# The y operands of an output projection moved into the weight strips' tiles, and w_out's raw tiles into a pool of their own

## The chip, the core and the metric

The kernel runs on one core of a Trainium2 chip. Its metric is the device time of one execution in microseconds (us); three runs stand behind the time before. The engines that matter are TensorE (PE in the profile; its weight loads are the row PEld), VectorE (DVE), ScalarE (ACT), GpSimd (POOL) and SyncE (SP), which issues every DMA of this kernel. Each engine takes its instructions in the order in which the program lists them, and SP issues its DMAs in the same way, so an instruction or a DMA that waits holds up those behind it on its engine.

## The reference

One encoder layer is applied to 1024 prompt tokens and to 256 sample tokens, each with 16 meta tokens in front. An input projection makes queries, keys, values and gates; eight heads attend globally and eight within a neighbourhood; the gated results are joined to `y` with 2048 features, and one output projection adds to the residual.

```python
def encoder_layer(h, norm_w, w_in, ..., w_out, rope_tabs):
    u = rms_norm(h, norm_w) @ w_in.astype(h.dtype)
    qa, ka, va, za, qb, kb, vb, zb = jnp.split(u, split_points(), axis=-1)
    ...
    ya = global_gqa(qa, ka, va) * jax.nn.silu(za)
    ...
    yb = neighbourhood_attention(qb, kb, vb, rpb) * jax.nn.silu(zb)
    y = jnp.concatenate([ya, yb], axis=-1) @ w_out.astype(h.dtype)
    return h + y
```

## The kernel before

Products in full precision are made from three matmuls on split operands: `split` (line 60) copies a float32 tile to a rounded half `hi` on ACT (L61) and writes what is left, `lo`, on DVE (L62); then hi·hi, hi·lo and lo·hi are accumulated in PSUM.

The input projection runs twice, over a first chunk of 512 tokens and over a second of 784 (`chunk1`, `chunk2`). In `strips` a column strip of 128 features of `w_in` is the stationary operand. It comes in four chunks, each of which is loaded to a raw tile and split to a tile `wh` and a tile `wl` of the pool `w` (tags `wh` and `wl`, four buffers each, 2 KB in a partition). The tokens `x` (split too, 16 tiles) are the moving operand. Each triplet L210, L211, L212 takes `wh`, `wh` and `wl` as stationary and x's `hi`, `lo`, `hi` as moving operand. Attention blocks run between strips; the last eight blocks of the neighbourhood heads are what remains of `local_blocks` when the last strip of the second chunk has been made, and they run during the first pass of the output projection.

The output projection (`outproj`) is Strassen-like: seven products (passes 1, 2, 5, 6, 7, 3, 4 in this order) of halves of `y` with halves of `w_out` or sums of them (`td`, made earlier). A pass has five token tiles `t` and two column blocks `b` of 512: ten steps `n`, each of 24 matmuls in `products` (L940, L941, L942: stationary yh, yh, yl; moving wh, wl, wh). So a pass has 240 matmuls and the seven have 1680, all 128x128 by 128x512.

- Stationary operands: `y_load` brings y for one token tile and `y_operand` splits it into a tile `yo` of 8 KB (hi and lo, 8 slices of 128 columns each), of which there are three. In passes 1, 2 and 4 the DMA (L889) writes y straight into the lo half of `yo`; the other passes load y halves to `yr` and add or subtract first (L904).
- Moving operands: `w_load` brings 2 KB rows of `w_out` (or of `td`) to raw tiles `ww` (L915, L917), which before use the eight buffers of tags `wh` and `wl`; `w_operand` splits each to one of 16 tiles `wm`.
- PSUM tiles `pq` are drained by `out_sums` on ACT (passes 1 and 5) and DVE.

Pools on the right side are stacked downward from the partition's end, the others upward. In the built program the tiles lie at these bytes of each partition: the `wh` and `wl` buffers at 11,008 to 27,391; x of the first chunk at 157,440 to 222,975; x of the second chunk from 120,576; `yo` at 118,528 to 143,103; `wm` at 143,232 to 208,767. The pools `us`, `wm` and `yo` take the room of the second chunk's x, so what is written there waits for matmuls of the last strip.

A scheduler orders each engine's instructions up to the end of the first pass of the output projection; what `in_order` records from the second pass on stays in the order in which the code is written.

Of the kernel before, what the change touches and what calls it, by code (L numbers as in the profile page):

```python
# [12 lines left out]
F32 = mybir.dt.float32  # L13
F32R = mybir.dt.float32r
# [6 lines left out]
P = 128  # L21
# [13 lines left out]
ALIGN = 128  # L35
# [9 lines left out]
WCH = 4  # L45
LAG = 6
TH = (NP + NS) // 2
NT = TH // P
FB = 512
# [5 lines left out]
class Kern:  # L55
# [824 lines left out]
    def y_load(self, p, t):  # L880

        def half(i, h):
            r = self.yr.tile([P, 8, P], F32, tag="yr", name="yr")
            self.nc.sync.dma_start(r[:], self.yd[i][:, NT * h + t])
            return r[:]

        if p in (1, 2, 4):
            r = self.yo.tile([P, 2, 8, P], F32R, tag="yo", name="yo", align_bytes=ALIGN)
            self.nc.sync.dma_start(r[:, 1].bitcast(F32), self.yd[p > 1][:, NT * (p == 4) + t])  # L889
            return r  # L890
        return [half(*x) for x in {7: [(0, 0), (0, 1)], 5: [(0, 1), (1, 1)], 6: [(0, 0)], 3: [(1, 0)]}[p]]

    def y_operand(self, p, t, r):
        nc = self.nc
        if p in (1, 2, 4):
            self.split(r[:, 0], r[:, 1], r[:, 1].bitcast(F32))
            return r
        if p == 7:
            v = r[0]
            nc.vector.tensor_tensor(out=v, in0=v, in1=r[1], op=ALU.subtract)  # L900
        else:
            v = self.ysum[t][:]
            a, b, op = {5: (r[0], r[-1], ALU.add), 6: (v, r[0], ALU.subtract), 3: (r[0], v, ALU.subtract)}[p]
            nc.vector.tensor_tensor(out=v, in0=a, in1=b, op=op)  # L904
        o = self.yo.tile([P, 2, 8, P], F32R, tag="yo", name="yo", align_bytes=ALIGN)
        self.split(o[:, 0], o[:, 1], v)
        return o

    def w_load(self, p, j):

        b, k = divmod(j, 8)
        src = {1: (0, 0), 2: (8, 0), 3: (8, FH)}.get(p)
        r = self.w.tile([P, FB], F32, tag=("wh", "wl")[j % 2], name="ww")
        if src is None:
            self.nc.sync.dma_start(r[:], self.td[p][:, k, FB * b:FB * b + FB])  # L915
        else:
            self.nc.sync.dma_start(r[:], self.io["w_out"][:, src[0] + k, src[1] + FB * b:][:, :FB])  # L917
        return r
# [15 lines left out]
    def products(self, ws, y):  # L934
        nc = self.nc
        ps = self.pq.tile([P, FB], F32, tag="pq", name="pq")
        for k in range(8):
            wh, wl = ws[k][:, 0, :], ws[k][:, 1, :]
            yh, yl = y[:, 0, k, :], y[:, 1, k, :]
            nc.tensor.matmul(ps[:], yh, wh, start=k == 0, stop=False)  # L940
            nc.tensor.matmul(ps[:], yh, wl, start=False, stop=False)  # L941
            nc.tensor.matmul(ps[:], yl, wh, start=False, stop=k == 7)  # L942
        return ps[:]
# [33 lines left out]
        self.nc.sync.dma_start(self.io["y"][:, NT * h + t, FH * c + FB * b:][:, :FB], o[:])  # L977

    def outproj(self, end_attention):
        self.U, self.V = {}, {}  # L980
        order = (1, 2, 5, 6, 7, 3, 4)
        N = 2 * NT * len(order)

        def step(n):
            q, r = divmod(n, 2 * NT)
            return order[q], *divmod(r, 2)

        def tile_of(m):
            return order[m // NT], m % NT

        M = NT * len(order)
        yr, ys, wr, ws, x, out = {}, {}, {}, {}, {}, {}

        def load_y(m):
            if m < M and m not in yr:
                yr[m] = self.y_load(*tile_of(m))

        def make_y(m):
            if m < M:
                load_y(m)  # L1000
                ys[m] = self.y_operand(*tile_of(m), yr.pop(m))

        def load_w(q, j):
            if q < len(order):
                wr[q, j] = self.w_load(order[q], j)

        def make_w(q, j):
            if q < len(order):
                ws[q, j] = self.w_operand(wr.pop((q, j)))

        make_y(0)
        for j in range(8):
            load_w(0, j)
        for j in range(16):
            make_w(0, j)
            if j < 8:
                load_w(0, 8 + j)
        traced = None
        for n in range(N):
            p, t, b = step(n)  # L1020
            q, m = n // (2 * NT), n // 2
            if n == 2 * NT - 1:
                for _ in self.blocks:
                    pass
            if n == 2 * NT:
                end_attention()
                traced = len(self.nc.cur_bb.bb.instructions)
                load_y(m + 1)
            if n - 2 in out:
                self.store(out.pop(n - 2), *step(n - 2))  # L1030
            last = t == NT - 1
            if t == NT - 2 and b == 0:
                for j in range(8):
                    load_w(q + 1, j)
            if q:
                for i in (n, n + 1, n + 2):
                    if i < N and i not in x:
                        x[i] = self.x_load(*step(i))
                load_y(m + 2)
            if b == 0 and (q or not last):  # L1040
                make_y(m + 1)
            if q == 0 and last and b == 1:
                make_y(m + 1)
            ps = self.products([ws[q, 8 * b + k] for k in range(8)], ys[m])
            if last:
                for k in range(8):
                    make_w(q + 1, 8 * b + k)
                    if b == 0:
                        load_w(q + 1, 8 + k)
            o = self.out_sums(p, 2 * t + b, ps, x.pop(n, None))  # L1050
            if o:
                out[n] = o
            if n < 2 * NT:
                next(self.blocks, None)
            if traced:
                traced = self.in_order(traced)
        for n in sorted(out):
            self.store(out[n], *step(n))

    def build(self):  # L1060
# [3 lines left out]
        with tc.tile_pool(name="dr", bufs=1, space=DRAM) as dp, tc.tile_pool(name="const", bufs=1) as cp, \  # L1064
# [19 lines left out]
            with ExitStack() as ps, ExitStack() as es_y:  # L1084
                def pool(stack, name, bufs, **kw):
                    setattr(self, name, stack.enter_context(tc.tile_pool(name=name, bufs=bufs, **kw)))
# [27 lines left out]
                es_pp.close()  # L1114
                pool(es_y, "pq", 4, space=PSUM, **kw)

                for name, bufs in (("us", 2 * NT), ("wm", 16), ("yo", 3)):
                    pool(es_late, name, bufs, side="right", **kw)

                def end_attention():  # L1120
# [96 lines left out]
```

## Time and profile before

| What | Value |
|---|---|
| median of three runs | 2192.64 us (2191.17 to 2193.61) |
| profiled execution: time, span of its instructions | 2193.63 us, 2191.8 us |
| mean granted TensorE clock | 0.997 |
| PE busy | 2165.2 us of the span |
| the 1680 matmuls of the output projection | from 1788.99 us to the end |
| the last matmul of the input projection starts at | 1767.65 us |

Times in the trace count from the span's start. A row of the timeline gives start, length, engine, line, operation and operands, and in brackets the idle time before it with what ended it; lengths of matmuls are latencies and overlap, so the pace is read from one start to the next. A row of the windows gives the stretch, its length, the busy time of each engine (instructions in brackets), the granted clock, the DMA share and the rate in GB/s.

### The profile page before, as it was taken

Reading aid. Unit: us, or ns where it says so; the run is one execution under the profiler, and the core shown is the slowest. Engines: PE = TensorE matmul, PEld = TensorE weight load, DVE = VectorE, ACT = ScalarE, POOL = GpSimd, SP = SyncE. Lnnn points to the kernel's source line nnn. Section 1 sums busy time; section 2 is a strip of 40 time slices with the busy share of each in tenths; the row PEclk is TensorE's granted clock in tenths of the full one; section 3 lists DMA queues with packets and bytes.
Section 4 is the critical chain, followed back from the end, with each engine's and each line's share of the span. In section 5 each row is a group of like instructions: output and inputs, shape, how many; then the busy total and the mean of one; then the engine's idle time right before and its main releaser. Section 6 shows DMA issues by size and latency. Waiting matters only on the chain.

```text
span 2191.8 us, 34025 instructions
## 1 busy us (share of the span) xinstructions
PE 2165.2 (99%) x11736; PEld 1881.7 (86%) x11736; DVE 1646.2 (75%) x2956; ACT 1124.4 (51%) x2259; POOL 518.2 (24%) x249
## 2 busy tenths in 40 slices
PE   8999999999999999999999999999999979999999
PEld 7888888888878999999999999999989968888887
DVE  8687976778774999995899998777768775546663
ACT  7556544554464667665676665444444454232220
POOL 1232421222212223322223323422323311000000
PEclk9999999999999999999999999999999989999999
DMA  8767898988364334334333336544434363653673
GB/s 297 221 196 229 280 307 303 345 275 264 129 220 143 106 108 116 106 107 143 104 111 116 98 122 188 167 139 137 133 123 134 95 235 113 221 190 125 218 228 113
DMA packets 262173, 383.82 MB, mean 175 GB/s; under 512 B 44880, under 2 KB 113136, under 8 KB 262000
## 3 DMA queue, kind: packets, MB, share of 16 engines
q1 hardware_dynamic: 262000, 381.65, 53.9%
q8 instruction: 92, 1.51, 0.3%
q14 instruction: 81, 0.66, 0.1%
HBM read 281.01 MB, written 100.38 MB: 174 GB/s over the span
## 4 chain that ended last, share of the span: by engine, by line
PE 94%; DVE 2%; DMA 2%; ACT 1%; issue 1%; SPq 0%; POOL 0%; DVEq 0%; ACTq 0%; POOLq 0%
PE pp L210 21%; PE pp L211 21%; PE pp L212 21%; PE pq L942 6%; PE pq L941 6%; PE pq L940 6%; PE po L470 2%; PE sp L438 1%; PE sp L333 1%; PE sp L334 1%; PE sp L332 1%; PE po L374 1%; PE po L372 1%; PE po L373 1%; DMA ww<-in_w_out 0%
## 5 line engine op out<-in xcount | busy, mean ns | idle before, releaser
L210 PE MATMUL pp<-x,wh 128*128 128x512 f32 (+1 forms) x2496 | 892.4, 359 | 7.3 <-ACT wh L61 5.5
L211 PE MATMUL pp<-x,wh 128*128 128x512 f32 (+1 forms) x2496 | 888.6, 356 | 0.4 <-DVE x L159 0.4
L212 PE MATMUL pp<-x,wl 128*128 128x512 f32 (+1 forms) x2496 | 888.7, 356 | 0.0
L210 PEld LDWEIGHTS pp<-x,wh 128*128 128x128 f32 x2496 | 469.1, 188 | 71.6 <-ACT wh L61 7.0
L212 PEld LDWEIGHTS pp<-x,wl 128*128 128x128 f32 x2496 | 469.6, 188 | 60.9 <-DVE wl L62 0.7
L211 PEld LDWEIGHTS pp<-x,wh 128*128 128x128 f32 x2496 | 469.9, 188 | 59.9 <-DVE x L159 1.3
L220 POOL PARTITION_ALL_REDUCE m<-ms x78 | 225.8, 2895 | 378.2 <-ACT ms L218 333.3
L62 DVE TENSOR_TENSOR wl<-wr,wh 128x512 fp32r<-128x512 f32 (+1 forms) x290 | 213.1, 738 | 130.3 <-ACT wh L61 105.3
L61 ACT CAST wh<-wr 128x512 fp32r<-128x512 f32 (+1 forms) x290 | 174.9, 607 | 224.6 <-PE pp L211 206.7
L301 POOL PARTITION_ALL_REDUCE tot<-a x80 | 178.2, 2228 | 470.2 <-DVE a L299 455.1
L940 PE MATMUL pq<-wm,yo 128*128 128x512 f32 x560 | 222.0, 396 | 0.0
L941 PE MATMUL pq<-wm,yo 128*128 128x512 f32 x560 | 221.3, 395 | 0.0
L942 PE MATMUL pq<-wm,yo 128*128 128x512 f32 x560 | 221.0, 395 | 0.0
L284 POOL PARTITION_ALL_REDUCE ma<-m x80 | 104.6, 1307 | 423.3 <-DVE m L282 415.1
L942 PEld LDWEIGHTS pq<-wm,yo 128*128 128x128 f32 x560 | 105.5, 188 | 24.8 <-DVE yo L62 0.4
L941 PEld LDWEIGHTS pq<-wm,yo 128*128 128x128 f32 x560 | 105.6, 189 | 24.6
L940 PEld LDWEIGHTS pq<-wm,yo 128*128 128x128 f32 x560 | 105.8, 189 | 24.3
L336 ACT COPY S<-sp 128x512 f32<-128x512 f32 x136 | 78.4, 579 | 51.2 <-PE sp L334 38.9
L194 ACT CAST wh<-wr 128x512 fp32r<-128x512 f32 x132 | 81.1, 614 | 41.5 <-PE pp L211 41.4
L62 DVE TENSOR_TENSOR pl<-S,ph 128x512 fp32r<-128x512 f32 x136 | 97.9, 732 | 3.9 <-ACT ph L61 3.8
L352 DVE TENSOR_TENSOR S<-S,ma 128x512 f32<-128x512 f32 x136 | 97.1, 772 | 3.9 <-POOL ma L284 3.9
L61 ACT CAST ph<-S 128x512 fp32r<-128x512 f32 x136 | 83.2, 612 | 32.9 <-PE po L373 32.3
(199 smaller groups left out, 3298.1 us busy)
## 6 DMA issues: line engine op xcount, KB each, us to landing
wr<-in_w_in SPq DMA_DIRECT2D x414, 256.0 KB, 3.5
wld<-wl SPq DMA_DIRECT2D x132, 256.0 KB, 4.4
wl<-wld SPq DMA_DIRECT2D x132, 256.0 KB, 3.1
wq<-in_w_out SPq DMA_DIRECT2D x64, 256.0 KB, 5.2
td<-wq SPq DMA_DIRECT2D x64, 256.0 KB, 4.3
ww<-td SPq DMA_DIRECT2D x64, 256.0 KB, 4.9
yr<-yd SPq DMA_DIRECT2D x30, 512.0 KB, 5.4
ww<-in_w_out SPq DMA_DIRECT2D x48, 256.0 KB, 5.3
```

The lines of the kernel that those rows point to most:

```text
L61: self.hi = nc.scalar.copy(hi, full).ins
L62: return nc.vector.tensor_tensor(out=lo, in0=full, in1=hi.bitcast(F32), op=ALU.subtract).ins
L210: nc.tensor.matmul(p[:, :n], wh[:, k, :], xh[:, :n], start=first, stop=False)
L211: nc.tensor.matmul(p[:, :n], wh[:, k, :], xl[:, :n], start=False, stop=False)
L212: nc.tensor.matmul(p[:, :n], wl[:, k, :], xh[:, :n], start=False, stop=last)
L220: nc.gpsimd.partition_all_reduce(m2[:], ms[:], P, RED.add)
L284: nc.gpsimd.partition_all_reduce(ma[:], m1[:], P, RED.max)
L301: nc.gpsimd.partition_all_reduce(tot[:], a1[:], P, RED.add)
L352: nc.vector.tensor_tensor(out=s, in0=s, in1=mb, op=ALU.subtract)
L940: nc.tensor.matmul(ps[:], yh, wh, start=k == 0, stop=False)
L941: nc.tensor.matmul(ps[:], yh, wl, start=False, stop=False)
L942: nc.tensor.matmul(ps[:], yl, wh, start=False, stop=k == 7)
```

## The change

Three things change, with no arithmetic of the outputs changed.

1. The stationary operand of the output projection no longer lies in `yo`. Each token tile's y is split into two `wh` tiles (hi) and two `wl` tiles (lo) of the pool `w`, four slices of 128 columns in each. With four buffers of each tag there is room for two token tiles, where `yo` had three. Each split of 128x1024 becomes two of 128x512, on ACT and on DVE: 35 more of each in the program.
2. In pass 1, and for the first tile of pass 2, y is loaded straight into two `wl` tiles (L890 of the changed file), with two DMAs of 256 KB in place of one of 512 KB. Passes 2 and 4 otherwise load y through `yr`.
3. The raw tiles of `w_out` get a pool of their own, `ww`, of eight buffers of 2 KB, where `yo` had been: at bytes 126,752 to 143,135.

```diff
--- before.py
+++ after.py
@@ -884,33 +884,42 @@
             self.nc.sync.dma_start(r[:], self.yd[i][:, NT * h + t])
             return r[:]
 
-        if p in (1, 2, 4):
-            r = self.yo.tile([P, 2, 8, P], F32R, tag="yo", name="yo", align_bytes=ALIGN)
-            self.nc.sync.dma_start(r[:, 1].bitcast(F32), self.yd[p > 1][:, NT * (p == 4) + t])
-            return r
-        return [half(*x) for x in {7: [(0, 0), (0, 1)], 5: [(0, 1), (1, 1)], 6: [(0, 0)], 3: [(1, 0)]}[p]]
+        if self.yr is None:
+            los = [self.w.tile([P, WCH, P], F32R, tag="wl", name="yl") for _ in range(2)]
+            for i, l in enumerate(los):
+                self.nc.sync.dma_start(l[:].bitcast(F32), self.yd[p > 1][:, t, WCH * i:WCH * i + WCH])
+            return los
+        return [half(*x) for x in {7: [(0, 0), (0, 1)], 5: [(0, 1), (1, 1)], 6: [(0, 0)], 3: [(1, 0)], 2: [(1, 0)], 4: [(1, 1)]}[p]]
 
     def y_operand(self, p, t, r):
         nc = self.nc
-        if p in (1, 2, 4):
-            self.split(r[:, 0], r[:, 1], r[:, 1].bitcast(F32))
-            return r
-        if p == 7:
+        if len(r[0].shape) == 3 and r[0].shape[1] == WCH:
+            his, los, full = [], r, [l[:].bitcast(F32) for l in r]
+            for l, f in zip(los, full):
+                his.append(self.w.tile([P, WCH, P], F32R, tag="wh", name="yh"))
+                self.split(his[-1][:], l[:], f)
+            return his, los
+        if p in (2, 4):
+            v = r[0]
+        elif p == 7:
             v = r[0]
             nc.vector.tensor_tensor(out=v, in0=v, in1=r[1], op=ALU.subtract)
         else:
             v = self.ysum[t][:]
             a, b, op = {5: (r[0], r[-1], ALU.add), 6: (v, r[0], ALU.subtract), 3: (r[0], v, ALU.subtract)}[p]
             nc.vector.tensor_tensor(out=v, in0=a, in1=b, op=op)
-        o = self.yo.tile([P, 2, 8, P], F32R, tag="yo", name="yo", align_bytes=ALIGN)
-        self.split(o[:, 0], o[:, 1], v)
-        return o
+        his, los = [], []
+        for i in range(2):
+            his.append(self.w.tile([P, WCH, P], F32R, tag="wh", name="yh"))
+            los.append(self.w.tile([P, WCH, P], F32R, tag="wl", name="yl"))
+            self.split(his[i][:], los[i][:], v[:, WCH * i:WCH * i + WCH])
+        return his, los
 
     def w_load(self, p, j):
 
         b, k = divmod(j, 8)
         src = {1: (0, 0), 2: (8, 0), 3: (8, FH)}.get(p)
-        r = self.w.tile([P, FB], F32, tag=("wh", "wl")[j % 2], name="ww")
+        r = self.ww.tile([P, FB], F32, tag="ww", name="ww")
         if src is None:
             self.nc.sync.dma_start(r[:], self.td[p][:, k, FB * b:FB * b + FB])
         else:
@@ -936,7 +945,7 @@
         ps = self.pq.tile([P, FB], F32, tag="pq", name="pq")
         for k in range(8):
             wh, wl = ws[k][:, 0, :], ws[k][:, 1, :]
-            yh, yl = y[:, 0, k, :], y[:, 1, k, :]
+            yh, yl = (a[k // WCH][:, k % WCH, :] for a in y)
             nc.tensor.matmul(ps[:], yh, wh, start=k == 0, stop=False)
             nc.tensor.matmul(ps[:], yh, wl, start=False, stop=False)
             nc.tensor.matmul(ps[:], yl, wh, start=False, stop=k == 7)
@@ -977,7 +986,7 @@
         self.nc.sync.dma_start(self.io["y"][:, NT * h + t, FH * c + FB * b:][:, :FB], o[:])
 
     def outproj(self, end_attention):
-        self.U, self.V = {}, {}
+        self.U, self.V, self.yr = {}, {}, None
         order = (1, 2, 5, 6, 7, 3, 4)
         N = 2 * NT * len(order)
 
@@ -1114,7 +1123,7 @@
                 es_pp.close()
                 pool(es_y, "pq", 4, space=PSUM, **kw)
 
-                for name, bufs in (("us", 2 * NT), ("wm", 16), ("yo", 3)):
+                for name, bufs in (("us", 2 * NT), ("wm", 16), ("ww", 8)):
                     pool(es_late, name, bufs, side="right", **kw)
 
                 def end_attention():
```

Line numbers of the changed file are 9 higher from `w_load` on (L917 there is L926, L940 is L949).

The scheduler makes another order of it around the end of the input projection. On SP, the rows from the last strip's end: in the program before, six raw loads of `w_out` (`ww`) stand ahead of the load of the next head's keys (`kfull`), and two more directly ahead of it.

```order
1220 L917 DMA ww<-in_w_out 128x512 x2
1221 L773 DMA zd_138<-zt 128x272
1222 L917 DMA ww<-in_w_out 128x512 x4
1223 L319 DMA yd_166<-y 128x4x64
1224 L917 DMA ww<-in_w_out 128x512 x2
1225 L778 DMA kfull<-kfd_78 128x240
1226 L779 DMA kfull<-k2d_148 128x784
1227 L780 DMA kfull<-kfd_78 128x16
1228 L789 DMA qfull<-qfd_122 128x240
1229 L790 DMA qfull<-q2d_164 128x784
```

In the changed program the same place on SP reads as follows (`yl` are the y loads; one more stands just ahead of these rows).

```order
1221 L773 DMA zd_138<-zt 128x272
1222 L890 DMA yl<-yd_165 128x512 x2
1223 L319 DMA yd_166<-y 128x4x64
1224 L926 DMA ww<-in_w_out 128x512 x3
1225 L778 DMA kfull<-kfd_78 128x240
1226 L779 DMA kfull<-k2d_148 128x784
1227 L780 DMA kfull<-kfd_78 128x16
1228 L494 DMA vn_88<-vl 128x4x128
1229 L478 DMA bt<-in_bt 128x1152
1230 L494 DMA vn_88<-vl 128x2x128
1231 L499 DMA vn_88<-vl 16x128
1232 L789 DMA qfull<-qfd_122 128x240
```

Three y loads stand where six raw loads stood, all raw loads come after the last strip, and the query load `qfull` stands behind the loads and stores of `vn` and `bt`.

On PE, the rows behind the last strip's transposes: before, the scores (`sp`) and the weighted sums (`po`) of attention come ahead of the first matmul of the output projection (`pq`).

```order
9513 L438 MATMUL sp<-qfull,kfull 128x128 x2
9514 L438 MATMUL sp<-qfull,kfull 128x192 x2
9515 L272 MATMUL sp<-q,km 112x256
9516 L273 MATMUL sp<-q,km 112x256
9517 L438 MATMUL sp<-qfull,kfull 128x128 x2
9518 L272 MATMUL sp<-q,km 112x256
9519 L273 MATMUL sp<-q,km 112x256
9520 L438 MATMUL sp<-qfull,kfull 128x192 x2
9521 L467 MATMUL po<-Pm,vm_271 128x256
9522 L470 MATMUL po<-S,vw 128x128 x2
9523 L470 MATMUL po<-S,vw 128x192 x2
9524 L940 MATMUL pq<-wm,yo 128x512
```

In the changed program nine of them, three slices of y, come first (the last four of the nine are shown), and these rows follow.

```order
9518 L951 MATMUL pq<-wm,yl 128x512
9519 L949 MATMUL pq<-wm,yh 128x512
9520 L950 MATMUL pq<-wm,yh 128x512
9521 L951 MATMUL pq<-wm,yl 128x512
9522 L438 MATMUL sp<-qfull,kfull 128x128 x2
9523 L438 MATMUL sp<-qfull,kfull 128x192 x2
9524 L467 MATMUL po<-Pm,vm_271 128x256
9525 L470 MATMUL po<-S,vw 128x128 x2
9526 L470 MATMUL po<-S,vw 128x192 x2
9527 L272 MATMUL sp<-q,km 112x256
9528 L949 MATMUL pq<-wm,yh 128x512
9529 L273 MATMUL sp<-q,km 112x256
```

The projection's matmuls have moved ahead of attention there and in between, and the block's weighted sums stand ahead of the next block's second scores.

On DVE, the softmax of the block whose weighted sums these are (`m` its maxima, `ma` their maximum over the partitions, `a` its sums, `Pm` its meta probabilities). Before:

```order
2404 L452 TENSOR_TENSOR m_20200<-S 128x256
2405 L62 TENSOR_TENSOR q<-qfull,q 128x1024
2406 L62 TENSOR_TENSOR wm<-ww,wm 128x512
2407 L455 TENSOR_TENSOR m_20200<-m_20200,S 128x128
2408 L62 TENSOR_TENSOR wm<-ww,wm 128x512 x2
2409 L282 TENSOR_TENSOR m_20200<-m_20200,Sm 16x256
2410 L276 SCALAR_TENSOR_TENSOR Sm<-sp,Sl 48x256
2411 L443 SCALAR_TENSOR_TENSOR S<-sp,bt 128x256
2412 L443 SCALAR_TENSOR_TENSOR S<-sp,bt 128x384
2413 L62 TENSOR_TENSOR wm<-ww,wm 128x512 x2
2414 L459 TENSOR_TENSOR S<-S,ma 128x256
2415 L462 TENSOR_TENSOR S<-S,ma 128x384
```

In the changed program:

```order
2406 L62 TENSOR_TENSOR wm<-ww,wm 128x512
2407 L282 TENSOR_TENSOR m_20200<-m_20200,Sm 16x256
2408 L62 TENSOR_TENSOR wm<-ww,wm 128x512
2409 L784 TENSOR_TENSOR km<-kfull,km 128x48
2410 L459 TENSOR_TENSOR S<-S,ma 128x256
2411 L462 TENSOR_TENSOR S<-S,ma 128x384
2412 L289 TENSOR_TENSOR Sm<-Sm,ma 48x256
2413 L452 TENSOR_TENSOR a_20214<-S 128x256
2414 L455 TENSOR_TENSOR a_20214<-a_20214,S 128x128
2415 L294 TENSOR_TENSOR Pm<-Sm,Pm 16x256
2416 L299 TENSOR_TENSOR a_20214<-a_20214,Sm 16x256
2417 L62 TENSOR_TENSOR q<-qfull,q 128x1024
```

The split of the next head's queries, which needs the `qfull` load, stood between the first two steps of this softmax (L452, L455) and now stands behind its last (L299).

## The prediction

> **What bounds the kernel now.** I read the page first, then the windows of the stretch in which PE is not full, then PE's timeline there, then its pace from one matmul's start to the next.
>
> ```profile
> span 2191.8 us, 34025 instructions
> PE 2165.2 (99%) x11736; PEld 1881.7 (86%) x11736; DVE 1646.2 (75%) x2956; ACT 1124.4 (51%) x2259; POOL 518.2 (24%) x249
> PE 94%; DVE 2%; DMA 2%; ACT 1%; issue 1%; SPq 0%; POOL 0%; DVEq 0%; ACTq 0%; POOLq 0%
> ```
>
> PE carries 94% of the chain that ended last, so only two things can move the time: PE's idle time, and the pace of its matmuls. The windows show where it idles.
>
> ```profile
> 1760.00:1780.00 20.00, 13.16 (x77) 11.65 (x75) 11.81 (x23) 9.55 (x20) 0.16 (x1) 0.83 0.69 226
> 1780.00:1800.00 20.00, 14.84 (x67) 12.59 (x68) 17.88 (x39) 11.23 (x22) 3.95 (x3) 0.83 0.90 329
> 1853.00:1909.00 56.00, 56.00 (x242) 45.40 (x242) 26.81 (x39) 13.43 (x20) 0.00 (x0) 1.00 0.58 193
> ```
>
> Between the last strip and the output projection PE misses 6.84 + 5.16 = 12.0 us, at a granted clock of 0.83 and with the DMA engines up to 0.90 busy. From 1853 us, in passes 2 to 7 of seven, PE is full at clock 1.00, and DVE (26.81 of 56) and ACT (13.43) have room. PE's rows of the gap:
>
> ```profile
> 1762.90 1.26 PE L470 MATMUL po<-S,vw 128*128 128x128 f32 x8
> ...
> 1771.90 0.55 PE L491 MATMUL tp<-ident,vt 128*128 128x128 f32 x3 [2.19 <-ACT vl L493]
> 1776.49 2.47 PE L438 MATMUL sp<-qfull,kfull 128*128 128x128 f32 x8 [4.05 <-DMA qfull<-q2d]
> ...
> 1781.87 0.68 PE L438 MATMUL sp<-qfull,kfull 128*128 128x128 f32 x4 [2.48 <-DVE S L443]
> ...
> 1786.73 0.58 PE L467 MATMUL po<-Pm,vm 128*128 128x256 f32 x1 [3.29 <-DVE Pm L294]
> 1787.11 2.33 PE L470 MATMUL po<-S,vw 128*128 128x128 f32 x8
> 1788.99 0.88 PE L940 MATMUL pq<-wm,yo 128*128 128x512 f32 x1
> ```
>
> Four stalls, 2.19 + 4.05 + 2.48 + 3.29 = 12.01 us, are the whole gap, and all stand ahead of the first `pq`. Then the pace, of the input projection (39 matmuls of 512 columns in a row, the last row being the first of the next kind) and of pass 2 (its first matmul and that of pass 3, 240 later):
>
> ```profile
> 405.22 0.39 PE L210 MATMUL pp<-x,wh 128*128 128x512 f32 x1
> ...
> 414.06 0.38 PE L210 MATMUL pp<-x,wh 128*128 128x496 f32 x1
> ```
> ```profile
> 1853.05 0.39 PE L940 MATMUL pq<-wm,yo 128*128 128x512 f32 x1
> ...
> 1908.81 0.39 PE L940 MATMUL pq<-wm,yo 128*128 128x512 f32 x1
> ```
>
> The first is 8.84 / 39 = 226.7 ns a matmul, the second 55.76 / 240 = 232.3 ns: the same shape, as many weight loads, the same order of hi and lo, the same distance of 2 KB between the moving hi and lo, but 5.7 ns more. What I find different is where the stationary operand lies: the strips' at 11 to 27 KB of the partition with x far above, `yo` at 119 to 143 KB just under `wm`.
>
> **The change part by part.**
>
> *Stationary operand.* After the change `yh` and `yl` lie in the very buffers of `wh` and `wl`, and `wm` stays within the range of x. If place sets the pace, `pq` should run as `pp`: passes 2 to 7 have 1440 matmuls, 1440 x 5.67 ns = 8.2 us, all on the path since PE is full there. The ends are 0 (place is nothing) and 8.2 for these passes; no stretch of 512-column matmuls in the trace is lastingly slower with the stationary operand low, so I see no loss. I take 8.2, since the nearest rows are those of the same buffers. Pass 1 shares PE with attention, after which the strips too need some ten matmuls to reach their pace, so of its 240 x 5.67 = 1.4 us I take 0.4 (ends 0 and 1.4).
>
> A rule of the Trainium skill speaks against this term: "TensorE: Matmul & The Clock Gate", section "Step-by-step: what each phase is for", says that PE has two independent read ports into SBUF, so that loading the next weights takes no read bandwidth from the running matmul; no place of an operand would then matter. The trace has two paces at one clock for one shape, which that rule does not explain.
>
> *The gap.* Before, y is loaded and split last of all:
>
> ```profile
> 1758.23 5.01 SPq L917 DMA_DIRECT2D ww<-in_w_out  x4
> ...
> 1767.88 0.80 SPq L917 DMA_DIRECT2D ww<-in_w_out  x2
> ...
> 1771.10 0.43 SPq L790 DMA_DIRECT2D qfull<-q2d  x1
> ...
> 1776.42 2.44 SPq L917 DMA_DIRECT2D ww<-in_w_out  x4
> ...
> 1780.55 0.45 SPq L889 DMA_DIRECT2D yo<-yd  x1
> ```
> ```profile
> 1774.72 0.42 DVE L452 TENSOR_TENSOR m<-S 128x256 f32<-128x256 f32 x1
> 1777.50 1.23 DVE L62 TENSOR_TENSOR q<-qfull,q 128x1024 fp32r<-128x1024 f32 x1 [2.36 <-ACT q L61]
> ...
> 1779.25 0.28 DVE L455 TENSOR_TENSOR m<-m,S 128x128 f32<-128x128 f32 x1
> ...
> 1788.23 1.57 DVE L62 TENSOR_TENSOR yo<-yo 128x1024 fp32r<-128x1024 f32 x1
> ```
>
> The y load goes out at 1780.55 and its lo half is ready at 1789.80, so no `pq` could fill a stall. And DVE holds the softmax of the block at work for 4.53 us (1774.72 to 1779.25) behind a split of q that waits for `qfull`; that softmax ends in the `Pm` on which the fourth stall waits. After the change the y loads take the places of six raw loads from 1753 us on, since `wl` tiles are free then; y is split before the strip ends; the q split stands behind the softmax; and `pq` matmuls stand between the pieces of attention. The third and fourth stalls then have work to cover them and one of their causes is gone: 2.48 + 3.29 = 5.77 us saved. The first two I leave at 6.24. Nine `pq` matmuls (2.1 us) fill part of the second, but `qfull` is now issued behind `vn` and `bt`, some 2 to 3 us later by the seven issues of about 0.4 us between. What is late next is `qfull`.
>
> Against it: all 16 raw loads now wait for the last strip (the old place of 1767.88), where six had gone before. At the rate of the gap's second window 256 KB take 0.80 us (262 KB / 329 GB/s), so six take 4.8; but five of the six y halves that were loaded in that crowd leave it or come later, which gives nearly as much back. So the ends of this part are -12.0 (all stalls filled) and +4.8 (raw loads simply late); I take -5.8, which the stalls' own rows carry.
>
> *The clock.* The eight L470 after the fourth stall take 2.33 us, those at 1762.90 took 1.26. With that stall filled they should run at full clock: 1.07, I take 1.0 (ends 0, and 2.5 with the slow L438 too).
>
> *Splits in halves, two y tiles in place of three.*
>
> ```profile
> L62 DVE TENSOR_TENSOR wm<-ww,wm 128x512 fp32r<-128x512 f32 x85 | 53.9, 687 | 6.3 <-ACT wm L61 6.0
> L61 ACT CAST wm<-ww 128x512 fp32r<-128x512 f32 x83 | 48.9, 620 | 19.7 <-DMA ww<-td 10.8 <-DMA ww<-in_w_out 3.6 <-PE pq L942 3.5
> L62 DVE TENSOR_TENSOR yo<-ysum,yo 128x1024 fp32r<-128x1024 f32 x15 | 18.4, 1226 | 40.5 <-ACT yo L61 40.5
> L61 ACT CAST yo<-ysum 128x1024 fp32r<-128x1024 f32 x15 | 15.7, 1049 | 89.0 <-DVE ysum L904 89.0
> yo<-yd SPq DMA_DIRECT2D x4, 512.0 KB, 3.6
> ```
>
> Two halves cost DVE 2 x 687 - 1226 = 148 ns more a tile and ACT 2 x 620 - 1049 = 191 ns: 35 tiles, 5.2 and 6.7 us, hidden in the room named above. With two tiles, y of tile t+1 can be written only when PE has left tile t-1, which leaves one tile's 48 matmuls, 11.2 us. In pass 1 the load waits as well: 3.6 + 1.24 + 1.37 = 6.2 us against 11.2. Later passes load to `yr` ahead. I take 0; a shallower buffer gives no gain, and without the cover it is at most the 6.2 us once in a pass. SP queues nothing new there but the y load itself, with stores of attention's y behind it, which nobody needs for two steps.
>
> *Sum.* -8.2 - 0.4 - 5.8 - 1.0 = -15.4 against the profiled execution's own 2193.6 (span 2191.8 and 1.8 around it; 1.0 above the median of 2192.64): 2178.2, so 2178 us. A measurement tells changes of about 0.2%, 4.4 us, from none.
>
> **The rivals.**
>
> - *Place is nothing.* Only the gap shrinks: 2193.6 - 6.8 = 2187. For it: attention's rows cannot be told apart by place, and something unseen may set the two paces. Against it: after each interruption the strips return to 226.7, and `pq` never does in 335 us. By the rule on the two ports this is what would come out. Chance 0.25.
> - *The pace alone.* The late raw loads eat what the filled stalls give: 2193.6 - 8.6 = 2185. For it: DMA share 0.90 in the gap. Chance 0.15.
> - *All stalls go.* -12.0 - 2.0 - 8.6: 2171. Against it: `qfull` comes later, and PE's first score needs it. Chance 0.05.
> - *Slower: raw weights behind the last strip, and no pace.* `ww` now lies where x was, so the first load waits for the strip's last matmuls; PE has `pq` matmuls ahead of attention in its order, so each late raw tile holds attention up too. Price +4.8: 2198. It decides when the sixteenth raw load lands later than its 24 matmuls can be fed, that is if the gap's DMA stays at 0.90 for over 5 us longer. Chance 0.08.
>
> **How the numbers follow.** The forecast as summed has 0.47. Around it I see 4 us either way (2174 to 2182). Taking in the rivals at 2185 and 2187 with as much uncertainty, and little beyond, 2172 to 2191 leaves out half of the rival at 2171 and the one at 2198, and the tails. Faster by over 0.2% (under 2188.3): 0.45 of the forecast, 0.16 of place-is-nothing, 0.11 of pace-alone and 0.05: 0.77. Slower: 0.05 of the last rival and 0.02 of tails: 0.07. The rest, 0.16, is within 0.2%.
>
> **What would show it.** The first matmuls of passes 2 and 3 should lie 54.4 us apart, not 55.8; passes 2 to 7 are then right. The first `pq` should start within 8 us of the last `pp`, with a stall on `qfull` and none on `Pm`; the two windows after the last strip should miss 6 us of PE, not 12. DVE's and ACT's splits of y must end no wait of PE in passes 2 to 7. A pace still at 232 ns refutes the first term; waits of `pq` for `wm` of more than 3 us refute the second.

## The result

The changed kernel took 2185.25 us (median of six executions, 2184.67 to 2187.12) against 2193.8 us of the kernel before (six executions, 2191.17 to 2194.68): a ratio of 0.9964, 95% interval 0.9954 to 0.9975. That is faster by some 8 us, and the forecast had 15.4: 2185 lies in the range, but the change is little more than half of what was forecast.

The profile after, first the page's head and chain, then the windows in the columns used before:

```profile
span 2183.9 us, 34132 instructions
PE 2164.4 (99%) x11736; PEld 1881.0 (86%) x11736; DVE 1647.3 (75%) x2991; ACT 1127.1 (52%) x2294; POOL 520.6 (24%) x249
PE 95%; DMA 1%; DVE 1%; ACT 1%; SPq 0%; issue 0%; POOL 0%; DVEq 0%; ACTq 0%; POOLq 0%
```

```profile
1760.00:1780.00 20.00, 14.55 (x79) 11.76 (x77) 12.23 (x28) 9.21 (x20) 5.16 (x3) 0.90 0.68 227
1780.00:1800.00 20.00, 20.00 (x93) 17.04 (x93) 17.33 (x37) 10.07 (x21) 3.19 (x2) 0.93 0.93 324
```

In the two windows behind the last strip PE now misses 5.45 us, where it missed 12.0. PE's rows of that stretch, and of the first matmuls of passes 2 and 3:

```profile
1769.59 0.52 PE L491 MATMUL tp<-ident,vt 128*128 128x128 f32 x3 [1.07 <-DVE vt L246]
1770.17 0.50 PE L949 MATMUL pq<-wm,yh 128*128 128x512 f32 x1
1770.90 0.50 PE L950 MATMUL pq<-wm,yh 128*128 128x512 f32 x1 [0.23 <-DVE wm L62]
...
1773.35 0.50 PE L950 MATMUL pq<-wm,yh 128*128 128x512 f32 x1 [0.30 <-DVE wm L62]
1773.69 0.40 PE L951 MATMUL pq<-wm,yl 128*128 128x512 f32 x1
1777.77 2.47 PE L438 MATMUL sp<-qfull,kfull 128*128 128x128 f32 x8 [3.68 <-DMA qfull<-q2d]
1779.78 0.67 PE L467 MATMUL po<-Pm,vm 128*128 128x256 f32 x1
1780.25 2.34 PE L470 MATMUL po<-S,vw 128*128 128x128 f32 x8
...
1845.34 0.39 PE L949 MATMUL pq<-wm,yh 128*128 128x512 f32 x1
...
1901.10 0.39 PE L949 MATMUL pq<-wm,yh 128*128 128x512 f32 x1
```

Of the four stalls two are gone, the one on `Pm` and the one on `S`; the first is 1.07 in place of 2.19, the one on `qfull` 3.68 in place of 4.05, and two short waits for `wm` are new: 5.28 us in all against 12.01. But passes 2 and 3 still begin 55.76 us apart, 232.3 ns a matmul. The pace did not move at all.

In what follows two lengths are read from each trace: from the start of the last `pp` to the start of pass 2 (the gap and pass 1), and from there to the start of the last matmul (passes 2 to 7). Before they are 85.40 and 334.63 us, after 78.88 and 334.39. So 6.5 us came from the gap and pass 1, and 0.2 from the rest. The last `pp` itself starts at 1766.46 after and 1767.65 before, but this moves between 1766.46 and 1768.27 over the runs below without order among them (e3_x128, which slows the strips, apart), so some 1 us of the profiled difference is scatter.

### The profile page after: what moved, and what is told of

It reads as the page before. It is cut to its first block, busy times and chain, and to the rows that moved or that the text cites. A ratio compares the mean times of both kernels' runs of the same rounds, so it can differ in the third digit from the quotient of the medians.

```text
span 2183.9 us, 34132 instructions
## 1 busy us (share of the span) xinstructions
PE 2164.4 (99%) x11736; PEld 1881.0 (86%) x11736; DVE 1647.3 (75%) x2991; ACT 1127.1 (52%) x2294; POOL 520.6 (24%) x249
## 4 chain that ended last, share of the span: by engine, by line
PE 95%; DMA 1%; DVE 1%; ACT 1%; SPq 0%; issue 0%; POOL 0%; DVEq 0%; ACTq 0%; POOLq 0%
PE pp L210 21%; PE pp L211 21%; PE pp L212 21%; PE pq L949 6%; PE pq L951 6%; PE pq L950 6%; PE po L470 2%; PE sp L438 2%; PE sp L333 1%; PE sp L334 1%; PE sp L332 1%; PE po L372 1%; PE po L374 1%; PE po L373 1%; PE tp L491 0%; DMA xr<-in_x 0%
## 5 line engine op out<-in xcount | busy, mean ns | idle before, releaser
L61 ACT CAST wh<-wr 128x512 fp32r<-128x512 f32 (+1 forms) x290 | 174.9, 607 | 226.7 <-PE pp L211 201.2
L949 PE MATMUL pq<-wm,yh 128*128 128x512 f32 x560 | 221.6, 396 | 0.2
L950 PE MATMUL pq<-wm,yh 128*128 128x512 f32 x560 | 220.9, 395 | 0.5 <-DVE wm L62 0.5
L951 PE MATMUL pq<-wm,yl 128*128 128x512 f32 x560 | 221.3, 395 | 0.0
L950 PEld LDWEIGHTS pq<-wm,yh 128*128 128x128 f32 x560 | 105.5, 188 | 25.7 <-DVE wm L62 1.4
L949 PEld LDWEIGHTS pq<-wm,yh 128*128 128x128 f32 x560 | 105.6, 189 | 25.0 <-ACT wm L61 0.9
L951 PEld LDWEIGHTS pq<-wm,yl 128*128 128x128 f32 x560 | 105.5, 188 | 24.4
```

The costliest lines, as they stand in the source:

```text
L61: self.hi = nc.scalar.copy(hi, full).ins
```

## Experiments on the pace

The forecast's first term rested on where y lies. It left open what else differs between the strips' matmuls and the projection's. The tiles' addresses, told with the kernel before, hold one more difference: every 512-column matmul of the strips has both its operands at a multiple of 256 bytes of the partition (x from 157,440 and 120,576, `wh` from 11,008), while in the projection `wm` starts at 143,232, an odd multiple of 128, and y at a multiple of 256 (118,528 before, 11,008 after).

**e1_wm256: the changed kernel with wm at a multiple of 256.**

```diff
-        w = self.wm.tile([P, 2, FB], F32R, tag="wm", name="wm", align_bytes=ALIGN)
+        w = self.wm.tile([P, 2, FB], F32R, tag="wm", name="wm", align_bytes=256)
```

> The changed kernel with one edit: the tiles wm (the moving operand of the output projection) start at a multiple of 256 bytes of the partition (143,104) and not at an odd multiple of 128 (143,232). In the program every 512-column matmul of the input projection has its moving operand at a multiple of 256, every one of the output projection at an odd multiple of 128. Theory A (this start sets the pace): the first matmuls of passes 2 and 3 lie 54.4 us apart, not 55.8; 1440 x 5.67 ns = 8.2 us and some 0.5 of pass 1 go: 2185.3 - 8.7 = 2176.5 us. Theory B (the pace comes of something in the stream itself, such as its groups of 24 matmuls or the traffic beside it): 55.8 us a pass, 2185 us.

Measured: 2177.45 us, ratio to the kernel before 0.9921 (0.9907 to 0.9934). The first matmuls of passes 2 and 3 on PE's timeline:

```profile
1845.72 0.39 PE L949 MATMUL pq<-wm,yh 128*128 128x512 f32 x1
...
1900.12 0.39 PE L949 MATMUL pq<-wm,yh 128*128 128x512 f32 x1
```

They are 54.40 us apart, 226.7 ns a matmul, and passes 2 to 7 take 326.17 us: 8.22 less, the size of the forecast's first term to a tenth, but for a move of 128 bytes in place of some 100 KB. Theory B falls.

**e2_before_wm256: the same edit in the kernel before.**

> The kernel before with the same edit; yo, which is stacked under wm, moves by 128 bytes too, so its stationary operands now start at an odd multiple of 128. Theory A, moving operand alone: 2193.8 - 8.7 = 2185 us, 54.4 us a pass, although y lies high in the partition. If the start of the stationary operand counted in the same way: 55.8 us a pass and 2194. Theory C (both the low place of y and the start of wm are needed): 2194, while the run on the changed kernel reaches 2176.5.

Measured: 2194.43 us, ratio 1.0004 (0.9995 to 1.0013).

```profile
1852.70 0.40 PE L940 MATMUL pq<-wm,yo 128*128 128x512 f32 x1
...
1908.70 0.40 PE L940 MATMUL pq<-wm,yo 128*128 128x512 f32 x1
```

56.00 us a pass, 233.3 ns a matmul. Since `yo` is stacked under `wm`, it had moved by 128 bytes too: `wm` at a multiple of 256, `yo` not. So the moving operand alone does not decide; either the stationary one counts in the same way, or a low place of y is needed as well. The next runs part these.

**e4_series: 19 series of 96 matmuls, one thing varied at a time.** After the kernel's end this is added (`low` are two tiles of the pool `w`, `top` two tiles at 223 KB, `g` the moving operand):

```diff
+            for j, (mo, so, d, n, high) in enumerate(SERIES):
+                for _ in range(4):
+                    ps = self.pq.tile([P, FB], F32, tag="pq", name=f"m{chr(97 + j)}")
+                    for i in range(24):
+                        k, r = divmod(i, 3)
+                        x = mo // 4 + 1024 * k + (d // 4 if r == 1 else 0)
+                        y = so // 4 + P * (k % 3)
+                        nc.tensor.matmul(ps[:, :n], flat[high][r // 2][:, y:y + P], g[:, x:x + n], start=i == 0, stop=i == 23)
```

> The changed kernel with 19 series of 96 matmuls each behind its end, in the form of the projection's (triplets hi, hi, lo over eight slices, groups of 24), in which one thing varies at a time: start of the moving operand (0, 128, 0, 64, 32, 192 bytes past a multiple of 256), start of the stationary operand (0, 128), its place (11 to 27 KB, 223 KB), the distance of moving lo from hi (2048, 2176 bytes), the columns (512, 496, 272, 256, 128). The time of the whole says nothing. Theory A: 226.7 ns a matmul with the moving operand at 0, 232.3 at 128, whatever the stationary operand's start and place; lo alone at 128 in between. Theory B: all series of 512 columns at one pace. My place theory: the series with stationary high at 232, low at 226.7, whatever the start.

A row of PE's timeline holds a whole series here, so from one start to the next are 96 matmuls. In order (`mb` on): moving at 128; 0; 64; 32; 192; stationary at 128; both at 128; both at 0 with y high; moving at 128 with y high; lo 128 bytes off; the last row closes it.

```profile
2223.79 22.55 PE L1089 MATMUL mb<-mv,st 128*128 128x512 f32 x96
2246.18 21.94 PE L1089 MATMUL mc<-mv,st 128*128 128x512 f32 x96
2267.95 22.15 PE L1089 MATMUL md<-mv,st 128*128 128x512 f32 x96
2289.94 22.55 PE L1089 MATMUL me<-mv,st 128*128 128x512 f32 x96
2312.33 22.56 PE L1089 MATMUL mf<-mv,st 128*128 128x512 f32 x96
2334.72 22.56 PE L1089 MATMUL mg<-mv,st 128*128 128x512 f32 x96
2357.12 21.94 PE L1089 MATMUL mh<-mv,st 128*128 128x512 f32 x96
2378.90 21.93 PE L1089 MATMUL mi<-mv,st 128*128 128x512 f32 x96
2400.67 22.55 PE L1089 MATMUL mj<-mv,st 128*128 128x512 f32 x96
2423.06 22.55 PE L1089 MATMUL mk<-mv,st 128*128 128x512 f32 x96
2445.45 21.61 PE L1089 MATMUL ml<-mv,st 128*128 128x496 f32 x96
```

By differences of starts over 96: moving at 128 past a multiple of 256 (`mb`) 233.2 ns, at 0 (`mc`) 226.8, at 64 (`md`) 229.1, at 32 and 192 (`me`, `mf`) 233.2; stationary at 128 alone (`mg`) 233.3; both at 128 (`mh`) 226.9. The place is nothing either way: with y high 226.8 where the starts agree (`mi`) and 233.2 where they don't (`mj`), with y low 226.8 and 233.2. Moving the lo half alone by 128 (`mk`) gives the slow pace too, 233.2, not one in between as theory A had it. So theory A needs another form: what counts is whether the two starts are equal modulo 256, for the moving hi and lo alike.

**e4b_series: other pairs of starts.** The same code with another list.

> The changed kernel with 18 other series of 96 matmuls behind its end; moving and stationary start past a multiple of 256, in pairs: 0 and 0, 256 and 0, 512 and 0, 0 and 256, 64 and 64, 32 and 32, 160 and 32, 64 and 192, 16 and 0, 96 and 0, 64 and 0, 160 and 0, 224 and 0, 0 and 64, 0 and 192; then 0 and 0 with lo 64 bytes further from hi, and 384 columns with 128 and 0, 0 and 0. The time of the whole says nothing. Equality modulo 256 as the rule: 226.7 ns for the first six (with 256 and 0 alike), 233 for 160 and 32 and for 64 and 192, between 227 and 233 for the others. If equality modulo 512 were the rule, 256 and 0 as well as 0 and 256 run at 233.

```profile
2226.29 21.92 PE L1089 MATMUL mb<-mv,st 128*128 128x512 f32 x96
2248.05 21.92 PE L1089 MATMUL mc<-mv,st 128*128 128x512 f32 x96
2269.81 21.92 PE L1089 MATMUL md<-mv,st 128*128 128x512 f32 x96
2291.57 21.97 PE L1089 MATMUL me<-mv,st 128*128 128x512 f32 x96
2313.38 21.95 PE L1089 MATMUL mf<-mv,st 128*128 128x512 f32 x96
2335.17 22.55 PE L1089 MATMUL mg<-mv,st 128*128 128x512 f32 x96
2357.56 22.46 PE L1089 MATMUL mh<-mv,st 128*128 128x512 f32 x96
2379.85 22.40 PE L1089 MATMUL mi<-mv,st 128*128 128x512 f32 x96
```

Moving and stationary at 256 and 0, 512 and 0, 0 and 256 (`mb`, `mc`, `md`): 21.76 us, 226.7 ns each, so equality modulo 512 is not needed. 64 and 64, 32 and 32 (`me`, `mf`): 227.2 and 227.0, a transient at their start included. 160 and 32, 64 and 192 (`mg`, `mh`), which differ by 128: 233.2 and 232.2. In the rows behind these the same list gives 231.7 at a difference of 16 bytes, 229.1 at 64, 233.4 at 96, 234.1 at 160, 233.2 at 192 and 233.4 at 224, and 232.1 with the lo half alone 64 bytes off. The first series of each list, which starts behind a long idle stretch, took 251.9 and 250.2 and is left out. In the other 25 series of 512 columns the fast pace goes with starts that are equal modulo 256, and with no others; only a difference of 64 between the two operands comes near it.

**e10_yo128: the kernel before, with yo moved down by 128 bytes.**

```diff
-                for name, bufs in (("us", 2 * NT), ("wm", 16), ("yo", 3)):
+                for name, bufs in (("us", 2 * NT), ("wm", 16), ("shift", 1), ("yo", 3)):
                     pool(es_late, name, bufs, side="right", **kw)
+                    if name == "shift":
+                        self.shift.tile([P, 32], F32, name="shift")
```

> The kernel before with one edit: yo moves down by 128 bytes (118,400 in place of 118,528), so that the stationary operand too starts at an odd multiple of 128, as wm does. Theory A, second form (what counts is that the starts of the two operands are equal modulo 256, from the series behind e4_series and from e2_before_wm256, where moving wm alone moved yo with it): 54.4 us a pass, 2193.8 - 8.7 = 2185 us, with y as high in the partition as before. Theory A, first form (the moving operand has to start at a multiple of 256): 2194. Theory C (a low place of y is needed too): 2194.

Measured: 2184.29 us, ratio 0.9957 (0.9944 to 0.9971).

```profile
1852.49 0.39 PE L940 MATMUL pq<-wm,yo 128*128 128x512 f32 x1
...
1906.89 0.39 PE L940 MATMUL pq<-wm,yo 128*128 128x512 f32 x1
```

54.40 us a pass with y as high as ever and both operands at odd multiples of 128. The second form of theory A holds in the kernel itself; the first form and theory C fall. All four pairs have now run at full length: `wm` and y at 128 and 0 (the kernels before and after) and at 0 and 128 (e2_before_wm256) are slow, 0 and 0 (e1_wm256) and 128 and 128 are fast. The spacer of 128 bytes is worth as much as the whole change under study.

**e3_x128: the strips of the first chunk made slow.**

```diff
+                    pool(es_1, "shift", 1, side="right")
+                    self.shift.tile([P, 32], F32, name="shift")
                     pool(es_1, "x", 16, side="right")
```

> The changed kernel with x of the first chunk moved by 128 bytes, so that 960 matmuls of 512 columns and 1536 of 496 in the input projection take their moving operand from odd multiples of 128 bytes; the second chunk (2496 of 512 columns) stays at multiples of 256, and so does the stationary operand. Theory A: the 960 go from 226.7 to 232.3 ns, 5.4 us, and the 1536 of 496 columns by 3 to 6 ns, 5 to 9 us: 2195 to 2200 us. Theory B: 2185.

Measured: 2194.92 us, 9.7 more than the changed kernel (ratio to the kernel before 1.0005, 0.9996 to 1.0014). The first row below is the first of a run of 512-column matmuls, the second its 37th:

```profile
407.69 0.40 PE L210 MATMUL pp<-x,wh 128*128 128x512 f32 x1
...
416.09 0.40 PE L210 MATMUL pp<-x,wh 128*128 128x512 f32 x1
```

36 matmuls take 8.40 us, 233.3 ns each, where the same stretch had 226.7. The last matmul of the first chunk starts at 616.77 us, where in the changed kernel it starts at 607.08: 9.7 us later, all of what was measured. From there to the last `pp` of the second chunk, which was not touched, it is 1159.6 us against 1159.4. The effect can be switched on where it was off as well as off where it was on.

## Experiments on the gap

**e5_raw_only: the raw tiles' pool alone, y high as before, two tiles.**

```diff
-        r = self.w.tile([P, FB], F32, tag=("wh", "wl")[j % 2], name="ww")
+        r = self.ww.tile([P, FB], F32, tag="ww", name="ww")
...
-                for name, bufs in (("us", 2 * NT), ("wm", 16), ("yo", 3)):
+                for name, bufs in (("us", 2 * NT), ("wm", 16), ("ww", 8), ("yo", 2)):
```

> The kernel before with the changed kernel's pool of eight raw tiles at the same bytes (126,752 to 143,135), and y in yo as before, two tiles deep in place of three, under it (110,336 to 126,720). The start of both operands modulo 256 stays as before (128 and 0), so the pace stays at 55.8 us a pass. On SP and DVE the order is that of the changed kernel (the split of q behind the softmax, raw loads behind the last strip), but y is loaded late, so no pq stands between the pieces of attention. Theory G1 (the gap shrinks because y is there early and pq matmuls fill it): the four stalls stay near 12 us, 2192 to 2198 us. Theory G2 (it shrinks because DVE's softmax no longer waits behind the split of q): the stall on Pm goes (3.3 us) and part of the one on S, 2188 to 2190 us. If both: 2190 with pq's first start some 3 us earlier than before.

Measured: 2201.79 us, ratio 1.0036 (1.0024 to 1.0049). The gap and pass 1 take 83.57 us, 1.8 less than before; passes 2 to 7 take 342.67, 8 more. PE's waits from 1850 us on (a row gives who waited for what, the us in total, how often, and the longest):

```profile
PE pq L940 <- ACT yo L61: 2.5, 2, 1.4
PE pq L942 <- DVE yo L62: 2.3, 3, 1.3
PE pq L941 <- DVE wm L62: 0.4, 2, 0.2
```

So two tiles are not free by themselves. Where y is loaded straight into the tile, the load waits for PE to leave it (the y loads of these passes, L889, wait 50.3 us for L942), and PE then waits for the splits. The rows hold 5.2 of the 8 us; where the rest goes, no row of waits shows. No stall on `Pm` is left in the gap, as G2 says, but that on `qfull` has grown to 8.78 us, and little is won: each theory held half.

**e12_raw_yr: the same with passes 2 and 4 loading y through yr.**

```diff
-        if p in (1, 2, 4):
+        if self.yr is None:
             r = self.yo.tile([P, 2, 8, P], F32R, tag="yo", name="yo", align_bytes=ALIGN)
...
+        if p in (2, 4):
+            v = r[0]
+        elif p == 7:
```

> e5_raw_only (yo high, two tiles deep, raw tiles in their own pool; 2201.8 us, of which some 8 us more than before in passes 2 to 7) with the changed kernel's way of loading y in passes 2 and 4, through yr. If the 8 us come of two tiles of y whose load waits for PE to leave them: passes 2 to 7 take 334.5 us again, 2193.5 us, and what is left beside the kernel before is the gap alone. If two tiles are too few anyhow: above 2197 us.

Measured: 2191.63 us, ratio 0.9989 (0.9980 to 0.9998). Passes 2 to 7 are back at 334.39 us, so the 8 us were the direct loads into two tiles, and `yr` covers them. The gap and pass 1 take 83.73 us; PE's waits in it:

```profile
PE sp L438 <- DMA qfull<-q2d: 8.6, 1, 8.6
PE sp L438 <- DVE S L443: 1.3, 1, 1.3
PE tp L491 <- DVE vt L246: 1.1, 1, 1.1
```

The order on DVE took the stall on `Pm` away, yet the stalls add up to 11.0 us, since `qfull`, now issued behind `vn` and `bt` (its second load at 1774.48, where before it went out at 1771.10), takes up what `Pm` gave.

**e13_ylate: the changed kernel with the loads of y late.** In pass 1 they are tied behind the eighth raw load on SP; `make_y(0)` moves behind the raw loads in the code for this.

```diff
-                self.nc.sync.dma_start(l[:].bitcast(F32), self.yd[p > 1][:, t, WCH * i:WCH * i + WCH])
+                with self.tc.issue_after(self.lastww):
+                    self.nc.sync.dma_start(l[:].bitcast(F32), self.yd[p > 1][:, t, WCH * i:WCH * i + WCH])
```

> The changed kernel with one thing undone: the loads of y in pass 1 are tied on SP behind the eighth raw load of w_out, so y is there late although its tiles are free early. Everything else stays: y low in the partition, two tiles deep, splits in halves, passes 2 and 4 through yr, raw tiles in their own pool. PE's order ahead of the first pq is then again that of the kernel before. Theory G1 (about 4.9 of the 6.5 us that the gap and pass 1 lost come of y being there early, the rest of the order on DVE and SP): from the last pp to pass 2 83.7 us as in e12_raw_yr, 2185.3 + 4.9 = 2190 us. If the low place or the halves themselves bring the 4.9 us: 78.9 us, 2185.3 us.

Measured: 2192.38 us, ratio 0.9996 (0.9987 to 1.0005). The gap and pass 1 take 84.90 us, so 6.0 of the 6.5 us are lost again, more than the 4.9 of G1, and the gain of the whole change is gone. PE's waits from 1760 us to 2190:

```profile
PE sp L438 <- DMA qfull<-q2d: 8.2, 1, 8.2
PE sp L438 <- DVE S L443: 1.7, 2, 1.3
PE tp L491 <- DVE vt L246: 1.1, 1, 1.1
PE pq L952 <- ACT yh L61: 0.8, 1, 0.8
```

The first loads of y go out at 1781.47 here, later still than in the kernel before (1780.55), and the last row, 0.8 us, is a wait for their split; so the 6.0 overstate the worth of early y a little, and 5 to 6 us is what e12_raw_yr, whose gap and pass 1 are 4.85 us longer than the changed kernel's, and this run bear out. In the changed kernel two of the loads stand in this row, ahead of the last `pp` at 1766.46:

```profile
1757.11 4.54 SPq L890 DMA_DIRECT2D yl<-yd  x2
```

What the low place buys is time, not pace: there y can be loaded while the last strip still reads x, and with y at hand PE has `pq` matmuls to do while `qfull` is on its way.

**e8_best: e1 with the raw tiles out of x's range.**

```diff
-                for name, bufs in (("us", 2 * NT), ("wm", 16), ("ww", 8)):
+                for name, bufs in (("us", 2 * NT), ("wm", 16), ("gap", 1), ("ww", 8)):
                     pool(es_late, name, bufs, side="right", **kw)
+                    if name == "gap":
+                        self.gap.tile([P, 5632], F32, name="gap")
```

> The changed kernel with wm at multiples of 256 (as in e1_wm256, 2177.5 us) and the raw tiles ww moved from x's range to 104,096 to 120,480, where no tile of the last strip lies, so that their loads need not wait for the last strip. On SP the loads of qfull now stand ahead of all raw loads. If the stall on qfull (3.68 us in the changed kernel) is the raw loads' doing, it falls by 2 to 3.5 us: 2174 to 2175.5. If qfull waits for its own data, it stays and raw tiles come later: 2177 to 2181. The pace is 54.4 us a pass by theory A in both forms.

Measured: 2180.67 us, ratio 0.9943 (0.9931 to 0.9956), and 80.47 us for the gap and pass 1, against 78.18 in e1_wm256. The scheduler now puts attention ahead of `pq` again and all raw loads behind `qfull`; PE waits 6.89 us for `qfull` with nothing to fill the time. The first score on `qfull` starts 10.5 us behind the last `pp`, where it was 11.5 in e1_wm256, and in both 5.0 us behind the issue of the second `qfull` load. So the three raw loads ahead of it on SP had held `qfull` up by 1 us at most, and the stall grew because no `pq` stands in it.

**e11_qk_first: e1 with the loads of kfull and qfull first on SP.**

```diff
-            nc.sync.dma_start(qf[:, :C1P], self.qfd[h][:])
-            nc.sync.dma_start(qf[:, C1P:], self.q2d[h][:])
+            with self.tc.high_priority(offset=100):
+                nc.sync.dma_start(qf[:, :C1P], self.qfd[h][:])
+                nc.sync.dma_start(qf[:, C1P:], self.q2d[h][:])
```

(and the three loads of `kfull` likewise)

> The changed kernel with wm at multiples of 256 (e1_wm256, 2177.5 us) and one edit more: the loads of kfull and qfull get a priority in the scheduler, so that on SP both stand ahead of vn and bt around the end of the input projection, as qfull did in the kernel before. If the place on SP sets the stall of the first score on qfull (3.3 us in e1_wm256, where four loads and stores of some 2.7 us stand ahead): the stall falls by 2 to 2.7 us, 2175 us. If qfull waits for its own data or for the transfers under way: 2177.5 us as in e1_wm256.

Measured: 2177.56 us, ratio 0.9931 (0.9919 to 0.9944): no better than e1_wm256. PE's two longest waits in the gap:

```profile
PE pq L951 <- DVE tot L310: 1.8, 1, 1.8
PE sp L438 <- DMA qfull<-q2d: 1.3, 1, 1.3
...
```

The stall on `qfull` fell from 3.3 to 1.3 us, by as much as its place on SP had let expect, and a new wait of 1.8 us on DVE gave most of it back: the gap and pass 1 take 77.23 us against 78.18, and a difference of 0.9 us is lost in the scatter of the runs. The fastest kernels of the study are thus e1_wm256 and this one, not to be told apart, 16 us below the kernel before.

## Why the prediction was right in part

- *The stationary operand, -8.2 and -0.4.* Wrong, and this is the failed step: "What I find different is where the stationary operand lies", and "If place sets the pace, `pq` should run as `pp`". Passes 2 to 7 gave 0.24 us (334.63 to 334.39), not 8.2, and the pace stayed at 232.3 ns. The two paces were real and the price of 8.2 us was right (8.22 in e1_wm256), but the cause is another: the starts of the two operands modulo 256, which the change left as they were. The addresses needed for it stood in the text; I compared them by kilobytes and not by their remainders.
- *The rivals and the range.* "Place is nothing" (2187) is the mechanism that the runs show. "The pace alone" (2185) hit the number by luck: it had the pace move and the gap give nothing, and the reverse happened. That 2185.25 lies in the range owes to these two rivals, not to the forecast's own working.
- *The rule against it.* The Trainium skill ("TensorE: Matmul & The Clock Gate", section "Step-by-step: what each phase is for") has two independent read ports for the moving and the stationary operand. Its outcome for this change was right, no gain from the place. It does not lead one to expect what the runs show: at one clock, one shape and one place the pace goes from 226.8 to 233.2 ns with the start of either operand and back to 226.9 with both, so the two operands' starts act together. Which part of the chip makes them do so, no run here shows.
- *The gap, -5.8.* Right, and for the reason given: the stalls on `S` and `Pm` are gone (5.77 us). Those that I left at 6.24 are 4.75, with 0.53 of new waits for `wm`, so that 6.73 us of idle time went, 0.96 more than forecast. `qfull` is what is late next, as said. Of the two causes named, early y carries 5 to 6 us (e12_raw_yr, e13_ylate); the order on DVE is alone worth 0.5 (e13_ylate) to 1.7 us (e12_raw_yr).
- *The clock, -1.0.* Did not come for the rows that it was read from: the eight L470 took 2.34 us after and 2.33 before. The forecast had them behind a stall that is filled; they now stand 2.5 us behind the start of the scores that waited for `qfull`, and the granted clock is 0.50 in the windows from 1776 to 1782 us. Before, it was 0.50 from 1774 to 1778 and once more from 1784 to 1790, so one of the two slow stretches went, but not the one that these rows are in now. The loss of idle time alone, 6.73 us, covers the 6.52.
- *Late raw loads, up to +4.8 (the slower rival).* Did not come: 0.53 us of waits for `wm`. e8_best, meant to take them out of x's range, does not test it, since the scheduler put them behind `qfull` there.
- *Two tiles of y and splits in halves, 0.* Right: PE waits for no y in passes 2 to 7, and a half costs DVE 688 ns, as reckoned. e5_raw_only shows what the cover by `yr` is worth: without it in passes 2 and 4, passes 2 to 7 are 8 us longer. My bound was 6.2 us once in a pass.
- *Sum.* Without the first term the working gives -15.4 + 8.6 = -6.8, and the traces' two lengths give -6.8 (6.52 + 0.24), with some 1 us of scatter ahead of the gap on top. That these agree to a tenth is luck in part: 0.96 us more idle time went than forecast, and the 1.0 of the clock did not come.

## What to carry to other kernels

Where a long row of equal matmuls keeps one pace and another row of the same shape a slower one at the same clock, compare the operands' start addresses modulo small powers of two as well as their places; in this kernel starts equal modulo 256 bytes were worth 5.7 ns of 232 a matmul, and a spacer of 128 bytes bought as much as a reworked allocation. A buffer that comes free earlier is worth the work that it lets the bottleneck do during someone else's wait; test such a claim by keeping the buffer and delaying its load. A stall that an earlier load shortens may come back as the next wait, so the time decides, not the stall.

## What was not expected of the hardware

- With 512 columns, PE's pace depends on the difference of the moving and the stationary operand's starts: 226.7 to 227.2 ns where it is a multiple of 256 bytes, 229.1 at 64, 231.7 to 234.1 at the other differences tried (e4_series and e4b_series). The Trainium skill ("SBUF — State Buffer", section "Operand start alignment") says of its rule on starts that it is about legality and not speed; the series here time them.
- Equality is not best for every shape. Of the further series of e4_series, 496 columns took 223.3 ns with equal starts and 226.5 with unequal ones, 272 columns 125.2 and 126.7, but 256 columns 119.8 and 118.6, one series of 96 of each (the third row below closes the second):

```profile
2512.81 11.66 PE L1089 MATMUL mp<-mv,st 128*128 128x256 f32 x96
2524.31 11.55 PE L1089 MATMUL mq<-mv,st 128*128 128x256 f32 x96
2535.70 10.83 PE L1089 MATMUL mr<-mv,st 128*128 128x128 f32 x96
```

- The slow pace is itself not one: at a difference of 128 bytes the kernel before ran at 232.3 ns and e2_before_wm256 at 233.3, each for whole passes on end. Why, was not tried.
